# Up projections of a two-layer diffusion backbone in groups of four output tiles, half of the row blocks by seven products of quarters

## The chip, the cores and the metric

One core of one Trainium2 chip runs the whole program. The metric is the device time of one execution in microseconds (us). The kernel before takes 1343.74 us, the median of three runs (1343.1 to 1344.23).

The engines are named as in the profile: PE is TensorE (matmul), PEld its weight loads, DVE VectorE, ACT ScalarE, POOL GpSimd, and SP the queue that issues most transfers.

## The reference

Two trunk layers work on 512 latent tokens of width 1024, the first also on 256 context tokens. Each layer is a mixer and then a gated channel mixer, and the change is in the channel mixer's first product (`w_up`, 1024 x 5632):

```python
def modulate(h, shift, scale):
    return h * (1.0 + scale[:, None, :]) + shift[:, None, :]

def conv_ffn(h, w_up, conv_w, conv_b, w_down):
    a, val = jnp.split(h @ w_up, 2, axis=-1)
    return (jax.nn.gelu(dwconv3(a, conv_w, conv_b), approximate=False) * val) @ w_down

for layer in range(2):
    mod = silu(c) @ ada_w[layer] + ada_b[layer]
    shift_m, scale_m, gate_m, shift_f, scale_f, gate_f = jnp.split(mod, 6, axis=-1)
    ...   # layer 0: neighbourhood attention and a gated recurrence; layer 1: a gated short convolution
    x = x + gate_m[:, None, :] * y
    h = modulate(rms_norm(x, norm_ffn_w[layer]), shift_f, scale_f)
    x = x + gate_f[:, None, :] * conv_ffn(h, ffn_w_up[layer], ...)
return rms_norm(x, final_norm_w)
```

All data is float32. `dwconv3` is a convolution of three taps along the tokens.

## The kernel before, in words

Everything is kept transposed: a tile has 128 features on the partitions and 512 tokens along the free axis, so that h is 8 tiles (`src[k]`, k = 0 to 7), each as a high part and a low part in fp32r. A product of float32 is made of three fp32r matmuls (`mm3`: high by high, weight high by low, weight low by high), and w_up is 22 output tiles for a and 22 for val.

`Weights` streams the weights. `_load` brings a chunk of 1 MB into one of two `wraw` buffers through the SP queue; `conv` makes from half a chunk (128x1024, one output tile) the high part by a cast on ACT (L84, `whi`, three buffers) and the low part by a subtraction on DVE (L85, `wlo`, three buffers). The plan fixes the order of the chunks, `ahead` how far the casts run in front of the matmuls.

`ffn_up` goes over j = 0 to 10, each time two tiles of a and two of val. For j = 0 `quad` does the four tiles in halves of 256 tokens, while the norm ahead still writes h. For the other ten, `pair` does two tiles of a (48 matmuls of 512 columns), then, after the convolution and gelu of a have been issued, `pair` does two of val. The convolution `conv3` is one activation on ACT (L1079, Identity with scale and bias) and two scalar_tensor_tensor on DVE (L1080, L1081), gelu is on ACT (L1108), the product with val on DVE (L1116), and `split` makes the high part (ACT, L242) and the low part (DVE, L243) that the down projection reads. All of these read PSUM directly. The accumulators are four PSUM banks that `acc_t` hands out in turn.

`units(n)` issues n small steps of the modulation vectors between the products: each `ada.unit` loads 256 KB of `ada_w` (`ar`, tag `araw`) and does one DVE instruction of 512 columns with it (L460, L462); every eighth is followed by a reduction (L466), a small matmul (L472) and four small additions (L478). There are 160 such steps in all. They are issued in `project_back`, in the up projections and in the odd mixer.

The Tile framework schedules the instructions of each engine within the order in which they are written and inserts the semaphores; each engine executes its own queue in order.

Of the kernel before, what the change touches and what calls it, by code (L numbers as in the profile page):

```python
# [9 lines left out]
F32 = mybir.dt.float32  # L10
# [8 lines left out]
P = 128  # L19
# [19 lines left out]
class Weights:  # L39


    def __init__(self, nc, pool, plan):
        self.nc, self.pool, self.plan = nc, pool, plan
        self.subs = [(c, s) for c, (_, subs) in enumerate(plan) for s in range(len(subs))]
        self.raw = {}
# [19 lines left out]
    def conv(self):  # L65

        if self.nsub >= len(self.subs):
            return
        c, s = self.subs[self.nsub]
        while self.nload <= min(c + 1, len(self.plan) - 1):  # L70
# [12 lines left out]
        rv = self.raw[c][i][:, k0:k1, c0:c1]  # L83
        self.nc.scalar.copy(hv, rv)  # L84
        self.pin(self.nc.vector.tensor_tensor(lv, rv, hv.bitcast(F32), ALU.subtract))  # L85
        self.ready.append((hv, lv))
        self.nsub += 1

    def ahead(self, n):
# [44 lines left out]
def backbone(ctx: ExitStack, tc: tile.TileContext, a, out, dump=None):  # L134
# [23 lines left out]
    def cols(w, c0):  # L158
        return [([ktiled(w)[:, :, c0 : c0 + 256]], [(0, 0, w.shape[0] // P, j, j + P) for j in (0, P)])]
# [21 lines left out]
        plan += cols(w_out, 256 * j)  # L181

    def ffn_up_plan(l):
        r = []
        for j in range(FT // 2):
            r += cols(up[l], 256 * j) + cols(up[l], FF + 256 * j)
        return r

    plan += ffn_up_plan(0)
# [51 lines left out]
    def split(hi, lo, src):  # L241
        S.copy(hi, src)  # L242
        V.tensor_tensor(lo, src, hi.bitcast(F32), ALU.subtract)  # L243
# [188 lines left out]
    class Ada:  # L432
# [560 lines left out]
    def project_back(nm, src, groups, gate, norm, start=0):  # L993
# [67 lines left out]
    def quad(nm, src, rest):  # L1061
# [13 lines left out]
        ws.pin = lambda i: i  # L1075
        return o[:2], o[2:]

    def conv3(t, src, w0, w1, w2, b):
        S.activation(t[:], src, AF.Identity, scale=w1, bias=b)  # L1079
        V.scalar_tensor_tensor(t[:, 1:], src[:, : T - 1], w0, t[:, 1:], ALU.mult, ALU.add)  # L1080
        V.scalar_tensor_tensor(t[:, : T - 1], src[:, 1:], w2, t[:, : T - 1], ALU.mult, ALU.add)  # L1081
# [8 lines left out]
    def units(n):  # L1090
        for _ in range(n):
            ada.unit(aux_t)

    def ffn_up(l, src, rest):
        g = []
        for j in range(FT // 2):
            if j == 0:
                oa, ov = quad(f"a{l}", src, rest)
            else:
                oa = pair(f"a{l}{j}", src)  # L1100
                units(1 + l)
            t = []
            for i in range(2):
                f = 2 * j + i
                col = lambda n: fcv[l][:, n : n + 1]
                tt = fp.tile([P, T], F32, tag="t", name=f"cv{l}{f}", bufs=5)
                conv3(tt, oa[i], col(f), col(22 + f), col(44 + f), col(66 + f))
                S.activation(tt[:], tt[:], AF.Gelu)  # L1108
                t.append(tt)
            if j:  # L1110
                ov = pair(f"v{l}{j}", src)
                units(1 + l)
            for i in range(2):
                f = 2 * j + i
                gh, gl = gtiles(l, f)
                V.tensor_tensor(ov[i][:], ov[i][:], t[i][:], ALU.mult)  # L1116
                split(gh, gl, ov[i][:])
                g.append((gh, gl))
        return g

    mix = [mixn[p_] for p_ in range(4)] + [mixg[h] for h in range(4)]
# [22 lines left out]
    for j in range(4):  # L1144
        if j == 0:
            oc, ou = quad("c", nrm.h, rest)
        else:
            oc = pair(f"c{j}", nrm.h)
            units(2)
        cs = []  # L1150
        for i in range(2):
            t = gp.tile([P, T], F32, tag=f"g{16 + i}", name=f"cs{j}{i}")
# [1 line left out]
            cs.append(t)  # L1154
        if j:
            ou = pair(f"u{j}", nrm.h)
            units(2)
        ts_ = []
        for i in range(2):
            m = 2 * j + i  # L1160
# [5 lines left out]
        units(2)  # L1166
# [18 lines left out]
    for k2 in range(2):  # L1185
        pt = aux_t(f"pgb{k2}")
        for k in range(4):
            dg = fp.tile([P, P], F32, tag="dg", name=f"dgb{k2}{k}", bufs=2)
# [60 lines left out]
def layout(inputs):  # L1249
# [4 lines left out]
                                "od_conv_w", "ada_b")]  # L1254
    for l in range(2):
        vecs += [inputs["ffn_conv_w"][l], inputs["ffn_conv_b"][l]]
    arrays["vec"] = np.ascontiguousarray(np.concatenate([np.asarray(v).reshape(-1, P) for v in vecs], 0).T)
    rpb = np.asarray(inputs["na_rpb"])[0].reshape(4, 2, 15, 31)
    rp = np.zeros((4, 15, 2, WPAD), rpb.dtype)
# [29 lines left out]
```

## Time and profile before

| what | value |
|---|---|
| median of three runs | 1343.74 us |
| the profiled execution's own time | 1343.25 us |
| its span, first to last instruction | 1341.5 us |
| busy share PE / PEld / DVE / ACT / POOL | 98 / 84 / 61 / 39 / 6 % |
| granted TensorE clock | 0.999 |
| up projections j = 1 to 10, layer 0 | 441.14 to 661.40 us of the span |
| the down projection of layer 0 behind them | 661.4 to 784.9 us |
| the odd mixer | 784.9 to 918.1 us |
| up projections j = 1 to 10, layer 1 | 985.90 to 1206.50 us |
| the down projection of layer 1 | 1206.5 to 1336 us |

The span is the execution as the profiler sees it; 1.75 us of the execution's time lie outside it. A row of a timeline has the start, the duration, the engine, the source line, what is written and read, and in brackets how long the engine was idle before and what released it. A row of the grouped views has busy time in all, the mean of one in ns, and the idle time before.

### The profile page before, as it was taken

Reading aid. Unit: us, or ns where it says so; the run is one execution under the profiler, and the core shown is the slowest. Engines: PE = TensorE matmul, PEld = TensorE weight load, DVE = VectorE, ACT = ScalarE, POOL = GpSimd, SP = SyncE. Lnnn points to the kernel's source line nnn. Section 1 sums busy time; section 2 is a strip of 40 time slices with the busy share of each in tenths; the row PEclk is TensorE's granted clock in tenths of the full one; section 3 lists DMA queues with packets and bytes.
Section 4 is the critical chain, followed back from the end, with each engine's and each line's share of the span. In section 5 each row is a group of like instructions: output and inputs, shape, how many; then the busy total and the mean of one; then the engine's idle time right before and its main releaser. Section 6 shows DMA issues by size and latency. Waiting matters only on the chain. (4 is left out here: it accounts for less than half of the span.)

```text
span 1341.5 us, 19127 instructions
## 1 busy us (share of the span) xinstructions
PE 1318.2 (98%) x7736; PEld 1126.1 (84%) x7736; DVE 821.3 (61%) x1354; ACT 527.9 (39%) x815; POOL 84.4 (6%) x87
## 2 busy tenths in 40 slices
PE   7999999999999999999999999999999999999997
PEld 4798888888779888888888898888988888889997
DVE  4668897887777655555566666557676444442333
ACT  4443445555544433333322243223543333333223
POOL 2204332311000000000000000000000000000000
PEclk9999999999999999999999999999999999999999
DMA  9842113674562333334366624445333233332231
GB/s 290 266 125 80 32 32 85 149 188 132 151 196 95 118 118 118 118 118 126 123 205 196 206 95 141 141 144 168 128 95 120 97 100 103 101 99 73 88 110 63
DMA packets 170825, 172.21 MB, mean 128 GB/s; under 512 B 14321, under 2 KB 144753, under 8 KB 170737
## 3 DMA queue, kind: packets, MB, share of 16 engines
q1 hardware_dynamic: 168736, 166.15, 40.1%
q10 hardware_dynamic: 2000, 4.85, 1.4%
q8 instruction: 60, 0.98, 0.3%
q14 instruction: 29, 0.23, 0.1%
HBM read 165.21 MB, written 2.10 MB: 125 GB/s over the span
## 5 line engine op out<-in xcount | busy, mean ns | idle before, releaser
L84 ACT CAST whi<-wraw 128x1024 fp32r<-128x1024 f32 (+1 forms) x202 | 207.7, 1031 | 469.2 <-PE ppv L247 93.4
L85 DVE TENSOR_TENSOR wlo<-wraw,whi 128x1024 fp32r<-128x1024 f32 (+1 forms) x202 | 243.5, 1207 | 217.8 <-ACT whi L84 216.5
L247 PE MATMUL ppa<-hf,whi 128*128 128x512 f32 (+1 forms) x448 | 161.6, 361 | 0.0
L246 PE MATMUL ppa<-hf,whi 128*128 128x512 f32 (+1 forms) x448 | 161.2, 360 | 0.0
L248 PE MATMUL ppa<-hf,wlo 128*128 128x512 f32 (+1 forms) x448 | 160.2, 358 | 0.0
L247 PE MATMUL ppv<-hf,whi 128*128 128x512 f32 x320 | 126.1, 394 | 0.0
L246 PE MATMUL ppv<-hf,whi 128*128 128x512 f32 x320 | 125.8, 393 | 0.0
L248 PE MATMUL ppv<-hf,wlo 128*128 128x512 f32 x320 | 124.3, 388 | 0.0
L462 DVE SCALAR_TENSOR_TENSOR aa<-ar,sil,aa 128x512 f32<-128x512 f32 x140 | 105.4, 753 | 17.4 <-DMA ar<-in_ada_w_dram 15.9
L1205 PE MATMUL pd<-whi,g 128*128 128x256 f32 x352 | 98.1, 279 | 0.0
L1207 PE MATMUL pd<-wlo,g 128*128 128x256 f32 x352 | 98.0, 278 | 0.0
L1206 PE MATMUL pd<-whi,g 128*128 128x256 f32 x352 | 97.7, 278 | 0.0
L246 PEld LDWEIGHTS ppa<-hf,whi 128*128 128x128 f32 x448 | 84.1, 188 | 13.9
L248 PEld LDWEIGHTS ppa<-hf,wlo 128*128 128x128 f32 x448 | 84.1, 188 | 13.2
L247 PEld LDWEIGHTS ppa<-hf,whi 128*128 128x128 f32 x448 | 84.2, 188 | 12.2
L1116 DVE TENSOR_TENSOR ppv<-ppv,cv 128x512 f32<-128x512 f32 x40 | 28.0, 700 | 86.0 <-PE ppv L248 86.0
L246 PE MATMUL pbd<-g,whi 128*128 128x512 f32 (+1 forms) x192 | 72.3, 377 | 0.0
L247 PE MATMUL pbd<-g,whi 128*128 128x512 f32 (+1 forms) x192 | 72.0, 375 | 0.0
L248 PE MATMUL pbd<-g,wlo 128*128 128x512 f32 (+1 forms) x192 | 71.7, 373 | 0.0
L246 PEld LDWEIGHTS ppv<-hf,whi 128*128 128x128 f32 x320 | 60.1, 188 | 13.8
L248 PEld LDWEIGHTS ppv<-hf,wlo 128*128 128x128 f32 x320 | 60.1, 188 | 13.4
L247 PEld LDWEIGHTS ppv<-hf,whi 128*128 128x128 f32 x320 | 60.2, 188 | 11.9
(340 smaller groups left out, 2862.3 us busy)
## 6 DMA issues: line engine op xcount, KB each, us to landing
wraw<-in_ffn_w_up_dram SPq DMA_DIRECT2D x44, 1024.0 KB, 5.1
ar<-in_ada_w_dram SPq DMA_DIRECT2D x160, 256.0 KB, 2.9
wraw<-in_ffn_w_down_dram SPq DMA_DIRECT2D x16, 1024.0 KB, 5.1
wraw<-in_od_w_in_dram SPq DMA_DIRECT2D x12, 1024.0 KB, 5.3
wraw<-in_ev_w_in_dram SPq DMA_DIRECT2D x20, 512.0 KB, 5.3
araw<-in_ada_w_dram SPq DMA_DIRECT2D x16, 512.0 KB, 6.5
wraw<-in_ffn_w_down_dram SPq DMA_DIRECT2D x8, 768.0 KB, 5.2
wraw<-in_ev_w_out_dram SPq DMA_DIRECT2D x4, 1024.0 KB, 7.3
```

Of the source, the lines that this page charges most:

```text
L84: self.nc.scalar.copy(hv, rv)
L85: self.pin(self.nc.vector.tensor_tensor(lv, rv, hv.bitcast(F32), ALU.subtract))
L246: TE.matmul(o, wh, mh, start=start, stop=False, skip_group_check=True)
L247: TE.matmul(o, wh, ml, start=False, stop=False, skip_group_check=True)
L248: TE.matmul(o, wl, mh, start=False, stop=stop, skip_group_check=True)
L462: pin(V.scalar_tensor_tensor(self.acc[:], raw[:], sil[:, r, 0:1], self.acc[:], ALU.mult, ALU.add))
L1116: V.tensor_tensor(ov[i][:], ov[i][:], t[i][:], ALU.mult)
L1205: TE.matmul(o[i][:, 0:256], gh[:, ts], w[0][:, k - k0], start=k == 0, stop=False)
L1206: TE.matmul(o[i][:, 0:256], gl[:, ts], w[0][:, k - k0], start=False, stop=False)
L1207: TE.matmul(o[i][:, 0:256], gh[:, ts], w[1][:, k - k0], start=False, stop=k == FT - 1)
```

## The change

For j = 1 to 10 `group` replaces the two `pair` calls. The four output tiles of one j are taken as two columns of a 2x2 block scheme: m = 0 and m = 1 are the two tiles of a and of val, the tokens are two halves (A: 0 to 255, B: 256 to 511), and the row blocks k = 0 to 3 are two pairs. The product of these quarters is done by seven products instead of eight, in Winograd's form, with sums of weights (S1 to S4) and sums of activations (T1 to T4). The row blocks k = 4 to 7 are done plainly, as W1 and W2 (the weights of m = 0 and m = 1) by XA and XB (the two halves of the activations). Each of the seven products is 12 matmuls of 256 columns, each of the four plain ones 24: 180 matmuls of 256 columns, where `pair` twice had 96 of 512.

The partial results share the banks a, b, c and d, and have to be combined: ACT copies bank contents to SBUF tiles `R` (L1180, eight copies of 128x256 for one j), and DVE adds other banks to them (L1176, eight of 128x256). Bank b is copied after S2·T2 while S3·T3 has still to be added to it. The convolution, gelu, product and split (now L1212, L1213, L1214, L1235, L1237, L281, L282) read and write R in SBUF.

The weights come from a new array `upq` that the host lays out: a chunk of quarters (A21, A22, A11, A12) and a chunk of W1 and W2. `_block` makes S3, S1, S2 and S4 on DVE (L105, L107, L109, L111; the last three in place in the raw tile), and casts and subtracts each (L122 on ACT, L123 on DVE). `differences` makes T2 to T4 once a layer, `first` T1. `units` moves: none in the up projections of layer 0, two after each of the groups j = 1 to 8 in layer 1, five instead of four in `project_back` where the rows come in several groups, and three instead of two in the odd mixer; `araw` has two buffers instead of three.

```diff
@@ Weights.conv, and the new _block
+        nm = self.plan[c][1][s]
+        while self.nload <= min(c + 1 + (nm == "W2"), len(self.plan) - 1):
             self._load()
+        if isinstance(nm, str):
+            self._block(c, nm)
+            return
...
+    HOME = {"A11": ("a", 0), "S1": ("a", 1), "A12": ("b", 0), "W1": ("c", None), "S2": ("d", 0), "S4": ("d", 1),
+            "S3": ("e", 0), "A22": ("e", 1), "W2": ("f", None)}
+    def _block(self, c, nm):
+        quarters = self.raw[c][0]
+        A21, A22, A11, A12 = (quarters[:, 0, 512 * i : 512 * i + 512] for i in range(4))
+        if nm == "S1":
+            s3 = self.pool.tile([P, 512], F32, tag="ws3", name=f"ws3{self.nsub}", bufs=1)
+            V.tensor_tensor(s3[:], A11, A21, ALU.subtract)
+            self.half["S3"] = s3[:]
+            V.tensor_tensor(A21, A21, A22, ALU.add)
+        elif nm == "S2":
+            V.tensor_tensor(A21, A21, A11, ALU.subtract)
+        elif nm == "S4":
+            V.tensor_tensor(A21, A12, A21, ALU.subtract)
...
+        if z in (None, 0):
+            self.half[key] = [self.pool.tile([P, 1024], F32R, tag=t, name=f"{t}{self.nsub}", bufs=3) for t in ("whi", "wlo")]
+        at = 512 * (z or 0)
+        hi, lo = (t[:, at : at + src.shape[-1]] for t in self.half[key])
+        self.nc.scalar.copy(hi, src)
+        V.tensor_tensor(lo, src, hi.bitcast(F32), ALU.subtract)
...
@@ ffn_up_plan
+        r = cols(up[l], 0) + cols(up[l], FF)
+        for j in range(FT // 2 - 1):
+            q = [a["upq"][l, j, i][:, None, :] for i in range(2)]
+            r += [([q[0]], ["A11", "S1", "A12", "W1", "S2", "S4", "S3", "A22", "W2"]), ([q[1]], [])]
@@ ada
-            raw = ap_.tile([P, T], F32, tag="araw", name=f"ar{n}", bufs=3)
+            raw = ap_.tile([P, T], F32, tag="araw", name=f"ar{n}", bufs=2)
-            while len(self.raw) < min(self.n + 3, 8 * len(self.jobs)):
+            while len(self.raw) < min(self.n + 2, 8 * len(self.jobs)):
@@ project_back
-                units(4)
+                units(4 if len(groups) == 1 else 5)
@@ the new group
+    def group(nm, mv):
+        bank = {n: acc_t(f"p{n}{nm}") for n in "bcad"}
+        R = [[fp.tile([P, T], F32, tag=t, name=f"R{nm}{t}", bufs=1) for t in ("sqa", "Rv")],
+             [fp.tile([P, T], F32, tag=t, name=f"R{nm}{t}", bufs=1) for t in ("r", "Rw")]]
...
+        upto(4)
+        product("b", "A11", "B11", True)
+        product("c", "S1", "T1", True)
+        copy("b", 0, A)
+        upto(5)
+        product("a", "A12", "B21", True)
+        copy("c", 1, B)
+        upto(7)
+        product("a", "W1", "XA", False, True)
+        upto(8)
+        product("c", "W1", "XB")
+        add("a", 0, A)
+        product("b", "S2", "T2")
+        upto(9)
+        product("c", "S4", "B22", False, True)
+        copy("b", 0, B)
+        product("b", "S3", "T3")
+        add("c", 0, B)
+        yield R[0]
+        upto(11)
+        add("b", 1, B)
+        product("b", "A22", "T4")
+        upto(12)
+        product("b", "W2", "XA", False, True)
+        product("d", "W2", "XB", True, True)
+        copy("b", 1, A)
+        add("d", 1, B)
+        yield R[1]
@@ ffn_up
-                oa = pair(f"a{l}{j}", src)
-                units(1 + l)
-                ov = pair(f"v{l}{j}", src)
-                units(1 + l)
+        for j in range(1, FT // 2):
+            for i, (ra, rv) in enumerate(group(f"{l}{j}", mv[0])):
+                gated_tile(2 * j + i, ra, rv)
+            if l and j < 9:
+                units(2)
```

`gated_tile` holds the convolution, gelu, product and split of one pair of tiles, as before. The other edits are the odd mixer's `units(3)`, one buffer instead of two for a tile `dg` of the last norm, the host's layout of `upq`, and a smaller scratch area for GpSimd's transfers.

In the order of PE, the place where bank b is copied and added to again reads as follows in the third group of layer 0 (T_4582 and T_4583 are T2 and T3, whi_5341/wlo_5342 hold S2 and then S4, whi_5362/wlo_5363 S3 and then A22, and whi_5310/wlo_5311 W1).

```order
L285 MATMUL pb_5302<-T_4582,whi_5341 128x256
L286 MATMUL pb_5302<-T_4582,whi_5341 128x256
L287 MATMUL pb_5302<-T_4582,wlo_5342 128x256
L285 MATMUL pb_5302<-T_4583,whi_5362 128x256
L286 MATMUL pb_5302<-T_4583,whi_5362 128x256
L287 MATMUL pb_5302<-T_4583,wlo_5363 128x256
...
L285 MATMUL pb_5302<-T_4583,whi_5362 128x256
L285 MATMUL pc_5303<-hf_4136,whi_5310 128x256
```

S3·T3 stands right behind S2·T2 in the same bank, seven of its twelve matmuls ahead of the 24 of W1·XB in bank c. In the kernel before, PE went from one bank to another at this place:

```order
L246 MATMUL ppv_5266<-hf_4141,whi_5188 128x512
L247 MATMUL ppv_5266<-hf_4141,whi_5188 128x512
L248 MATMUL ppv_5266<-hf_4141,wlo_5189 128x512
L246 MATMUL ppv_5267<-hf_4134,whi_5256 128x512
L247 MATMUL ppv_5267<-hf_4134,whi_5256 128x512
```

Nothing between these rows had to be copied first. On ACT, the rows around the same place of the changed kernel follow; R02 belongs to the group before, R03 to this one, and cv_5293 and g_5298 are the gated tile of the group before.

```order
L1180 COPY R02r<-pb_5041 128x256
L1180 COPY R02Rw<-pb_5041 128x256
L1212 ACTIVATE cv_5293<-R02r,vec 128x512
L122 CAST whi_5362<-ws_5218 128x512
L122 CAST whi_5362<-wraw_5169 128x512
L122 CAST whi_5341<-wraw_5169 128x512
L1235 ACTIVATE cv_5293<-cv_5293 128x512
L1180 COPY R03r<-pc_5303 128x256
L281 CAST g_5298<-R02Rw 128x512
L1180 COPY R03sqa<-pb_5302 128x256
L1180 COPY R03Rv<-pb_5302 128x256
```

The two copies of bank b in the last rows stand behind the whole gated tile of the group before and the cast L281 of its product. On ACT before, a cast of weights and a step of the gated tile took turns:

```order
L84 CAST whi_5329<-wraw_5186 128x1024
L242 CAST g_5319<-ppv_5266 128x512
L84 CAST whi_5335<-wraw_5260 128x1024
L242 CAST g_5324<-ppv_5267 128x512
L84 CAST whi_5404<-wraw_5260 128x1024
L1079 ACTIVATE cv_5394<-ppa_5339,vec 128x512
```

On DVE, this is what stands ahead of the product R02Rw that the cast L281 reads, and what follows it:

```order
L111 TENSOR_TENSOR wraw_5169<-wraw_5169 128x512
L1214 SCALAR_TENSOR_TENSOR cv_5293<-R02r,vec,cv_5293 128x511
L123 TENSOR_TENSOR wlo_5363<-ws_5218,whi_5362 128x512
L123 TENSOR_TENSOR wlo_5342<-wraw_5169,whi_5341 128x512
L1237 TENSOR_TENSOR R02Rw<-R02Rw,cv_5293 128x512
L123 TENSOR_TENSOR wlo_5363<-wraw_5169,whi_5362 128x512
L1176 TENSOR_TENSOR R03sqa<-pa_5304,R03sqa 128x256
L282 TENSOR_TENSOR g_5298<-R02Rw,g_5298 128x512
L1176 TENSOR_TENSOR R03Rv<-pa_5304,R03Rv 128x256
L105 TENSOR_TENSOR ws_5480<-wraw_5430 128x512
L123 TENSOR_TENSOR wlo_5433<-wraw_5212,whi_5432 128x1024
```

The product L1237 comes behind the difference S4 and two low parts, and the next chunk's quarters (wraw_5430) stand ahead of W2's low part. Before, DVE had one low part of 128x1024 for each product:

```order
L1116 TENSOR_TENSOR ppv_5266<-ppv_5266,cv_5246 128x512
L85 TENSOR_TENSOR wlo_5330<-wraw_5186,whi_5329 128x1024
L243 TENSOR_TENSOR g_5320<-ppv_5266,g_5319 128x512
L1116 TENSOR_TENSOR ppv_5267<-ppv_5267,cv_5251 128x512
L85 TENSOR_TENSOR wlo_5336<-wraw_5260,whi_5335 128x1024
L243 TENSOR_TENSOR g_5325<-ppv_5267,g_5324 128x512
```

There, one low part of the weights stands between two steps of the gated tiles.

More of the change, by code (lines that the diff above doesn't have):

```diff
@@ L44, in __init__ @@
         self.subs = [(c, s) for c, (_, subs) in enumerate(plan) for s in range(len(subs))]
+        self.half = {}
         self.raw = {}
@@ L86, in conv @@
         self.ready.append((hv, lv))
+        self.nsub += 1
+    HOME = {"A11": ("a", 0), "S1": ("a", 1), "A12": ("b", 0), "W1": ("c", None), "S2": ("d", 0), "S4": ("d", 1),
+            "S3": ("e", 0), "A22": ("e", 1), "W2": ("f", None)}
+    def _block(self, c, nm):
+        V = self.nc.vector
+        quarters = self.raw[c][0]
[9 more added lines that the diff above has]
+            V.tensor_tensor(A21, A12, A21, ALU.subtract)
+        if nm in ("W1", "W2"):
+            at = 1024 * (nm == "W2")
+            src = self.raw[c + 1][0][:, 0, at : at + 1024]
+        else:
+            src = {"A11": A11, "A12": A12, "A22": A22, "S3": self.half.get("S3")}.get(nm, A21)
+        key, z = self.HOME[nm]
+        if z in (None, 0):
[4 more added lines that the diff above has]
+        V.tensor_tensor(lo, src, hi.bitcast(F32), ALU.subtract)
+        self.ready.append(tuple(t.rearrange("p (g k c) -> p g k c", g=2, c=P) for t in (hi, lo)))
         self.nsub += 1
@@ new lines, in group, with product, upto, add @@
+    def group(nm, mv):
+        bank = {n: acc_t(f"p{n}{nm}") for n in "bcad"}
+        v = {n: t[:].rearrange("p (g t) -> p g t", g=2) for n, t in bank.items()}
+        R = [[fp.tile([P, T], F32, tag=t, name=f"R{nm}{t}", bufs=1) for t in ("sqa", "Rv")],
+             [fp.tile([P, T], F32, tag=t, name=f"R{nm}{t}", bufs=1) for t in ("r", "Rw")]]
+        base = ws.ncall
+        order = ["A11", "S1", "A12", "W1", "S2", "S4", "S3", "A22", "W2"]
+        w = {}
+        A, B = HALF
+        def product(n, wn, xn, first=False, last=False):
+            while wn not in w:
+                w[order[len(w)]] = ws.get(0)
+            wh, wl = w[wn]
+            nk = wh.shape[2]
+            for g_ in range(2):
+                for k in range(nk):
+                    mh, ml = mv[xn](k)
+                    mm3(v[n][:, g_], wh[:, g_, k], wl[:, g_, k], mh, ml, first and g_ == 0 and k == 0,
+                        last and k == nk - 1)
+        def upto(n):
+            ws.ahead(base + n - ws.ncall)
+        def add(n, m, c):
+            for g_ in range(2):
+                r = R[m][g_][:, c]
+                V.tensor_tensor(r, v[n][:, g_], r, ALU.add)
+        def copy(n, m, c):
+            for g_ in range(2):
+                S.copy(R[m][g_][:, c], v[n][:, g_])
+        upto(4)
[26 more added lines that the diff above has]
+        yield R[1]
@@ L1095, in ffn_up, with gated_tile, before @@
         g = []
[L1096 to L1099, printed above, removed]
-                oa = pair(f"a{l}{j}", src)
-                units(1 + l)
[L1102 to L1110, printed above, removed]
-                ov = pair(f"v{l}{j}", src)
-                units(1 + l)
[L1113 to L1118, printed above, removed]
+        mv = []
+        def gated_tile(f, oa, ov):
+            col = lambda n: fcv[l][:, n : n + 1]
+            tt = fp.tile([P, T], F32, tag="t", name=f"cv{l}{f}", bufs=5)
+            conv3(tt, oa, col(f), col(22 + f), col(44 + f), col(66 + f))
+            S.activation(tt[:], tt[:], AF.Gelu)
+            gh, gl = gtiles(l, f)
+            V.tensor_tensor(ov[:], ov[:], tt[:], ALU.mult)
+            split(gh, gl, ov[:])
+            g.append((gh, gl))
+        def before():
+            rest()
+            mv.extend(differences(l, src))
+        oa, ov = quad(f"a{l}", src, before)
+        mv[1]()
+        for i in range(2):
+            gated_tile(i, oa[i], ov[i])
+        for j in range(1, FT // 2):
[3 more added lines that the diff above has]
+                units(2)
         return g
```

44 lines of the change are left out of this document (35 added, 9 removed).

## The prediction, made before the changed kernel was run

> **What bounds the kernel now.** I read the page's first section, then the busy time of each engine by stretches, then the timelines of PE, DVE and ACT in the third group of layer 0 (times in us).
>
> ```profile
> span 1341.5 us, 19127 instructions
> PE 1318.2 (98%) x7736; PEld 1126.1 (84%) x7736; DVE 821.3 (61%) x1354; ACT 527.9 (39%) x815; POOL 84.4 (6%) x87
> ```
>
> The second row gives busy time, share and instructions: PE is nearly always busy. By stretches (length; then busy time and instructions of PE, PEld, DVE, ACT and POOL, granted clock, DMA share, GB/s):
>
> ```profile
> 441.14:661.40 220.26, 220.26 (x968) 180.83 (x967) 122.80 (x161) 82.25 (x107) 0.00 (x0) 1.00 0.39 122
> 985.90:1206.50 220.60, 220.60 (x970) 181.13 (x969) 117.76 (x150) 82.85 (x108) 0.00 (x0) 1.00 0.33 107
> 661.40:784.90 123.50, 123.50 (x590) 102.96 (x589) 79.48 (x121) 35.22 (x43) 0.00 (x0) 1.00 0.63 201
> ```
>
> In the two stretches that the change rewrites PE has no gap at all, and DVE works 122.80 of 220.26 us. So one j costs 22.04 us (the mean of 22.03 and 22.06), and whatever takes matmuls away gains, if the rest keeps up. The durations of PE follow, first of 512 columns, then of 256 (the quad):
>
> ```profile
> 463.35 0.39 PE L246 MATMUL ppa<-hf,whi 128*128 128x512 f32 x1
> 474.34 0.39 PE L246 MATMUL ppv<-hf,whi 128*128 128x512 f32 x1
> ...
> 428.54 0.28 PE L248 MATMUL ppa<-hf,wlo 128*128 128x256 f32 x1
> 439.99 0.28 PE L248 MATMUL ppa<-hf,wlo 128*128 128x256 f32 x1
> L246 PEld LDWEIGHTS ppa<-hf,whi 128*128 128x128 f32 x448 | 84.1, 188 | 13.9
> ```
>
> Between the first two lie 48 matmuls: 10.99/48 = 0.229 each. Between the next two lie 99: 11.45/99 = 0.1157, a little over half. A matmul of 256 columns is recorded for 0.28, so its result is there 0.16 after the next could start.
>
> **The change, PE first.** Out go 96 matmuls of 512 columns for each j, in come 180 of 256: 180 x 0.1157 = 20.83, 1.21 less than 22.04. Over 20 groups that is 24 us, if PE never waits. Whether it waits is decided by ACT and DVE, which have one queue each. Their prices, from the timelines (idle time and releaser in brackets) and from the groups (busy, mean ns | idle):
>
> ```profile
> 475.39 1.22 DVE L85 TENSOR_TENSOR wlo<-wraw,whi 128x1024 fp32r<-128x1024 f32 x1 [2.82 <-ACT whi L84]
> 476.53 0.74 DVE L1080 SCALAR_TENSOR_TENSOR cv<-ppa,vec,cv 128x511 f32<-128x511 f32 x1
> 477.19 0.74 DVE L462 SCALAR_TENSOR_TENSOR aa<-ar,sil,aa 128x512 f32<-128x512 f32 x1
> 477.85 0.74 DVE L1081 SCALAR_TENSOR_TENSOR cv<-ppa,vec,cv 128x511 f32<-128x511 f32 x1
> 480.03 0.70 DVE L1116 TENSOR_TENSOR ppv<-ppv,cv 128x512 f32<-128x512 f32 x1 [1.44 <-PE ppv L248]
> 487.52 0.69 DVE L243 TENSOR_TENSOR g<-ppv,g 128x512 fp32r<-128x512 f32 x1
> 488.12 0.74 DVE L462 SCALAR_TENSOR_TENSOR aa<-ar,sil,aa 128x512 f32<-128x512 f32 x1
> ...
> 474.31 1.05 ACT L84 CAST whi<-wraw 128x1024 fp32r<-128x1024 f32 x1 [1.01 <-PE ppa L247]
> 478.69 0.63 ACT L1108 ACTIVATE cv<-cv 128x512 f32<-128x512 f32 x1 [2.65 <-DVE cv L1081]
> ...
> 479.60 0.39 PE L248 MATMUL ppv<-hf,wlo 128*128 128x512 f32 x1
> L1212 DVE TENSOR_TENSOR yt<-pd,gb 128x256 f32<-128x256 f32 x16 | 6.5, 421 | 18.5 <-PE pd L1207 18.5
> L1079 ACT ACTIVATE cv<-ppa,vec 128x512 f32<-128x512 f32 x44 | 34.1, 775 | 18.0 <-PE ppa L248 18.0
> L586 ACT COPY ckt<-pkc 128x256 f32<-128x256 f32 x8 | 3.0, 371 | 28.2 <-PE pkc L584 28.2
> L242 ACT CAST QS<-qn 64x512 fp32r<-64x512 f32 x8 | 4.9, 617 | 0.2
> ```
>
> On DVE the next instruction starts about 0.08 before the record of the last ends: 1.14 for 1024 columns, 0.66 for a scalar_tensor_tensor of 511, 0.60 for a tensor_tensor of 512 (487.52 to 488.12), and by the same cut 0.34 for 256 (421 ns recorded). On ACT, by the same cut of about 0.09, it is 0.28 for a copy of 256 columns (371) and 0.53 for a cast of 512 (617). Handing over: ACT to DVE 0.03 (475.36 to 475.39), DVE to ACT 0.10 (478.59 to 478.69), PE to DVE 0.04 (479.99 to 480.03).
>
> Per group DVE has two low parts of 1024, fifteen tensor_tensors of 512 (seven lows, four differences, two products, two splits), four scalar_tensor_tensors and eight adds of 256: 2.28 + 9.00 + 2.64 + 2.72 = 16.6, against 12.28 a j before (122.80/10), which included the steps of the modulation vectors. It fits into 20.8 as a sum. ACT likewise stays under two thirds. So no engine is the bound; the order within the queues is.
>
> **Where PE waits.** S3·T3 adds to bank b, so its first matmul must wait for the two ACT copies R03sqa and R03Rv of that bank. They stand behind cast L281 of the last group's product, which waits for DVE's L1237. I put zero at the start of the last matmul of the previous group's W2·XA and follow the queues as they are ordered:
>
> - DVE: W1's low part waits for that matmul to free its buffer, 0.28 + 0.04 = 0.32, next at 1.46. S2's low part to 2.06.
> - ACT: a cast of 512 from 0.20 to 0.73 (its buffer is freed by W2's last high part), the two copies of bank b to 1.29, identity L1212 to 2.07.
> - DVE: first scalar_tensor_tensor from 2.10, S4 from 2.76, second from 3.36, low part of S3 from 4.02, of S4 from 4.62, L1237 from 5.22, recorded to 5.92. (Gelu, from 4.11 + 0.10 to 4.84 on ACT, is in time.)
> - ACT: cast L281 at 6.01, the copies at 6.51 and 6.79, ended at 7.16. PE may start S3·T3 at 7.20.
> - PE: one matmul of S1·T1, 12 of A12, 24 of W1·XA, 12 of S2·T2 lie between, so it is free at 50 x 0.1157 = 5.79.
>
> PE waits 1.41. Had ACT been free, the copies would still cost 0.16 + 0.04 + 0.28 + 0.37 + 0.04 = 0.9 here: that is the floor of this term, 1.41 the value I take, since every step of it has its row.
>
> The Trainium skill speaks to this, in "Perfetto Trace Analysis", section Optimizing Tensor Performance: independent groups of matmuls should rotate through PSUM banks, so that emptying one overlaps the next, and larger matmuls are better than smaller ones. The trace before agrees (banks alternate and PE has no gap), and no run here yet shows the other case. By that rule the change goes wrong exactly at S3·T3; with a bank of its own the sum would be 1.41 a group less.
>
> Two smaller waits follow. DVE's first difference L105 of the next group waits for the quarters, and W2's low part stands behind it. The raw tile is free when A22's low part is done, 5.82 + 0.69 = 6.51; the transfer then takes as long as this one of the same size:
>
> ```profile
> wraw<-in_ffn_w_up_dram SPq DMA_DIRECT2D x44, 1024.0 KB, 5.1
> ```
>
> So it lands at 6.53 + 5.1 = 11.63; L105 to 12.25, W2's low part ends 13.48. PE wants it 52 matmuls after 7.20, at 13.22: it waits 0.3. The second half of the low part for S1 stands behind two adds, one low part, two scalar_tensor_tensors, L107 and an add: DVE reaches it at about 16.93 and ends it at 17.62; PE wants it at 17.43: 0.2. All the rest of what is added (differences, other copies and adds, split) ends ahead of its reader by 0.1 or more, or is read a group later. The bounds of these two: nothing if the quarters, now in rows of 8 KB where they were of 1 KB, land 0.9 sooner; later than 5.1 is the second rival below.
>
> One group: 20.83 + 1.41 + 0.3 + 0.2 = 22.75, against 22.04. Twenty groups: +14.2. With 0.1135 to 0.118 for a matmul and 0.9 to 2.2 of waits it is 21.3 to 23.4, -14 to +28.
>
> **The other parts.** The first group behind each quad inherits its tiles:
>
> ```profile
> 441.18 0.75 DVE L1080 SCALAR_TENSOR_TENSOR cv<-ppa,vec,cv 128x511 f32<-128x511 f32 x1 [8.01 <-ACT cv L1079]
> 443.73 1.28 ACT L1108 ACT_TABLE_LOAD   x1
> ```
>
> DVE idles 8 us inside the quad, which covers `differences` (on DVE four sums, three low parts of 512 and eight differences of 256: 7 x 0.60 + 8 x 0.34 = 6.9). Behind the quad two identities, four scalar_tensor_tensors, the table load of 1.28 and two products now stand ahead of the first group's low parts: I reckon 2 us a layer, +4, between 0 and +8. In the down projection of layer 0 five steps of the modulation vectors for four, on two buffers instead of three:
>
> ```profile
> DMA to landing us min/median/max: 2.6/3.0/6.4
> DVE aa L462 <- DMA ar<-in_ada_w_dram: 15.9, 17, 2.4
> ```
>
> The first row is that stage's; with three buffers DVE already waited 17 times for a step's data over the span, 2.4 at most. DVE has 44 of 123.5 us to spare there, and PE waits only where it uses this up: 0 to +5, I take +1. The steps removed from layer 0's up projections free DVE for nothing that PE wanted, and those moved into layer 1's fall where DVE waits for quarters. In the odd mixer DVE keeps its spare time, and `dg` is a moment: both nothing.
>
> Sum: 14.2 + 4 + 1 = +19.2 on the profiled execution's own 1343.25 (span 1341.5 and 1.75 around it; the median of the runs is 0.5 higher): 1362.5, about 1.4% slower.
>
> **Rivals.**
>
> - *The count of matmuls decides* (faster). PE sees fewer of these waits than I reckoned: if the waits of a group stay under 22.04 - 20.83 = 1.21, it gains. With only the floor of 0.9 it is 21.73, -6; with the scheduler's overlap perfect, -24; with 2 to 4 us of the quads, 1321 to 1341, most likely 1335. For it: my chain of nine steps need only be 0.3 shorter than I think, and the two small waits vanish with a faster transfer. Against it: each step has its row, and the queues run in order.
> - *The quarters come late* (slower still). Their raw tile is freed only after S4 and A22 have been used, so the transfer can't run ahead. If it takes 6.4 (the slowest landing of a step's 256 KB, above) instead of 5.1, DVE passes 1.3 on to W2's low part in every group: 20 x 1.3 = 26 more, 1388. For it: DVE reads the tile first in its queue. Against it: 5.1 is the median of 44.
> - *Weight loads bound the smaller matmuls.* 180 loads of 0.188 (the row of PEld) would make 33.8 a group, (33.8 - 22.04) x 20 = +235, 1579. Against it: in the quad each matmul of 256 columns has its load, and they are 0.1157 apart. The Trainium skill, "TensorE: Matmul & The Clock Gate", section Back-to-back issue gap, says that the spacing is set by load and matmul together, pipelined; the quad shows that here they overlap.
>
> **How the numbers follow.** The forecast, 1347 to 1382, has 0.58; the gain 0.26; late quarters 0.09; bound by loads 0.01; and 0.06 is left for no change. The measurement can tell about 0.2% from nothing, 2.7 us. So faster 0.26, same 0.06, slower 0.68. For the range I leave out what lies above 1384 (late quarters, loads) and the best part of the gain, below 1328.
>
> **What would show it.** In the profile after: 180 matmuls a group at 0.115 to 0.116; a gap of PE at the first matmul of S3·T3, released by ACT's copy R..Rv, of 0.9 to 1.5, twenty times; smaller gaps at W2 into bank d, released by DVE's low part, whose own wait is for L105's transfer; a group of 22.3 to 23.2. I am wrong if the gap at S3·T3 is under 0.9 or lies elsewhere, if the quarters land well under 5 us, or if the first groups and the down projection take more than 8 us together.

## The result and the profile after

The changed kernel takes 1374.82 us (median of four runs, 1372.33 to 1376.03), the kernel before 1343.42 (four runs): a ratio of 1.0231, interval 1.0214 to 1.0249. It is slower by 31.4 us; 19.2 were forecast, and the forecast's range, 1347 to 1382, holds the time. One of the twelve executions of the last kernel in the experiments below took 1596.78 us at a granted clock of 0.752, and the time given there leaves it out. The first lines of the page after:

```profile
span 1372.8 us, 23237 instructions
PE 1320.2 (96%) x9416; PEld 1196.2 (87%) x9416; DVE 969.7 (71%) x1728; ACT 629.7 (46%) x1085; POOL 83.6 (6%) x87
```

PE's busy time hardly changed although matmul columns were saved (a record of 256 columns is 0.28 long where the next starts after 0.12, so that a wait of less than 0.16 shows as no gap), and PE's share fell from 98 to 96%. The stretches that answer to those before (columns as there): the groups of layer 0, its down projection, the odd mixer, and the groups of layer 1.

```profile
445.28:674.27 228.99, 218.10 (x1810) 214.65 (x1809) 172.60 (x295) 128.32 (x232) 0.00 (x0) 1.00 0.26 92
674.27:806.44 132.17, 125.86 (x588) 103.60 (x586) 84.53 (x130) 36.64 (x46) 0.00 (x0) 0.99 0.63 203
806.44:941.80 135.36, 134.28 (x684) 114.06 (x683) 93.00 (x150) 43.91 (x62) 0.00 (x0) 1.00 0.49 151
1009.76:1240.00 230.24, 219.89 (x1824) 216.05 (x1823) 181.69 (x318) 128.40 (x232) 0.00 (x0) 1.00 0.28 100
```

PE now has gaps in all four. The start of the quad of layer 0 tells that something was lost even ahead of the groups; the first row is of the kernel before, the second of after:

```profile
418.43 0.28 PE L246 MATMUL ppa<-hf,whi 128*128 128x256 f32 x1
422.50 0.28 PE L285 MATMUL ppa<-hf,whi 128*128 128x256 f32 x1
```

By stages, each from its first matmul, as in such rows (before, the down projection goes from 661.58 to 785.01 and the odd mixer to 918.29; after, 1.18 us of the down projection stand inside the groups of layer 0 and are counted with it):

| stage | forecast | measured |
|---|---|---|
| up to the quad of layer 0 | 0 | +4.1 |
| groups of layer 0, with the first | +9.1 | +7.4 |
| down projection of layer 0 | +1 | +9.9 |
| odd mixer | 0 | +2.1 |
| its output projection and the quads | 0 | +0.4 |
| layer 1 from the groups to the end | +9.1 | +7.4 |
| span | +19.2 | +31.3 |

The last row but one is known to about 3 us only: the last down projection takes 127.6 us in the kernel before and 131.0 and 128.3 in the first two of the experiments, which change nothing in its products. The groups came out near what was worked out, and half of the loss, 16.5 of 31.3 us, lies elsewhere. The third group of layer 0, in the timelines of DVE, ACT and PE:

```profile
498.20 0.69 DVE L1237 TENSOR_TENSOR R02Rw<-R02Rw,cv 128x512 f32<-128x512 f32 x1
504.35 0.69 DVE L105 TENSOR_TENSOR ws<-wraw 128x512 f32<-128x512 f32 x1 [3.59 <-DMA wraw<-in_upq_dram]
...
498.92 0.62 ACT L281 CAST g<-R02Rw 128x512 fp32r<-128x512 f32 x1 [0.85 <-DVE R02Rw L1237]
499.45 0.37 ACT L1180 COPY R03sqa<-pb 128x256 f32<-128x256 f32 x1
499.71 0.38 ACT L1180 COPY R03Rv<-pb 128x256 f32<-128x256 f32 x1
...
498.72 0.28 PE L287 MATMUL pb<-T,wlo 128*128 128x256 f32 x1
500.14 0.39 PE L285 MATMUL pb<-T,whi 128*128 128x256 f32 x1 [1.14 <-ACT R03Rv L1180]
```

With the prediction's zero at 492.95, L1237 starts at 5.25 (5.22 forecast) and S3·T3 at 7.19 (7.20). PE starts nothing for 1.42 us, 1.30 more than a matmul takes. This stands in nine groups of layer 0 and in six of layer 1; three more of layer 1 have a gap of 0.6 to 0.9 us there, and the first group of each layer has none. The copies that end one group and start the next give the period; the first and the last of eight:

```profile
493.68 0.36 ACT L1180 COPY R02r<-pb 128x256 f32<-128x256 f32 x1
653.59 0.36 ACT L1180 COPY R09r<-pb 128x256 f32<-128x256 f32 x1
```

159.91/7 = 22.84 a group, 22.75 forecast. In layer 1 the same copies are 22.80 to 22.89 us apart four times and then 23.20 to 23.61 four times; what adds the half microsecond there stays open.

### The profile page after: what moved, and what is told of

Read it like the earlier page. It is cut to its first block, busy times and chain, and to the rows that moved or that the text cites. A ratio compares the mean times of both kernels' runs of the same rounds, so it can differ in the third digit from the quotient of the medians.

```text
span 1372.8 us, 23237 instructions
## 1 busy us (share of the span) xinstructions
PE 1320.2 (96%) x9416; PEld 1196.2 (87%) x9416; DVE 969.7 (71%) x1728; ACT 629.7 (46%) x1085; POOL 83.6 (6%) x87
## 5 line engine op out<-in xcount | busy, mean ns | idle before, releaser
L89 ACT CAST whi<-wraw 128x1024 fp32r<-128x1024 f32 (+1 forms) x122 | 124.1, 1021 | 279.0 <-PE pbd L286 70.2
L90 DVE TENSOR_TENSOR wlo<-wraw,whi 128x1024 fp32r<-128x1024 f32 (+1 forms) x122 | 144.9, 1190 | 106.0 <-ACT whi L89 102.0
L122 ACT CAST whi<-wraw 128x512 fp32r<-128x512 f32 (+1 forms) x160 | 116.5, 729 | 139.2 <-PE pc L286 69.3
L123 DVE TENSOR_TENSOR wlo<-wraw,whi 128x512 fp32r<-128x512 f32 (+1 forms) x160 | 129.5, 821 | 49.7 <-PE pb L287 32.3
L287 PE MATMUL pc<-hf,wlo 128*128 128x256 f32 x320 | 91.1, 285 | 0.7 <-DVE wlo L123 0.7
L285 PE MATMUL pc<-hf,whi 128*128 128x256 f32 x320 | 89.3, 279 | 0.0
L286 PE MATMUL pc<-hf,whi 128*128 128x256 f32 x320 | 89.3, 279 | 0.0
L285 PE MATMUL pb<-T,whi 128*128 128x256 f32 x240 | 69.2, 288 | 19.3 <-ACT R05Rv L1180 1.1
L287 PE MATMUL pa<-hf,wlo 128*128 128x256 f32 x240 | 67.4, 281 | 0.9 <-DVE wlo L123 0.9
L285 PE MATMUL pb<-hf,whi 128*128 128x256 f32 x240 | 67.8, 283 | 0.0
L286 PE MATMUL pb<-T,whi 128*128 128x256 f32 x240 | 67.2, 280 | 0.0
L286 PE MATMUL pb<-hf,whi 128*128 128x256 f32 x240 | 67.1, 280 | 0.0
L285 PE MATMUL pa<-hf,whi 128*128 128x256 f32 x240 | 67.1, 280 | 0.0
L286 PE MATMUL pa<-hf,whi 128*128 128x256 f32 x240 | 67.0, 279 | 0.0
```

Of the source, the lines that this page charges most:

```text
L122: self.nc.scalar.copy(hi, src)
L285: TE.matmul(o, wh, mh, start=start, stop=False, skip_group_check=True)
L286: TE.matmul(o, wh, ml, start=False, stop=False, skip_group_check=True)
L287: TE.matmul(o, wl, mh, start=False, stop=stop, skip_group_check=True)
```

## The experiments

All are timed against the kernel before on the same chip; ratios with their 95% interval. Beside the changed kernel the kernel before took 1343.42 us, beside the runs below 1343.88 to 1346.15, so a difference of 1 or 2 us from the changed kernel is better read from the ratios. The runs ask two things: where the loss outside the groups comes from, and what sets the period inside.

**Two buffers alone.** The kernel before, with

```diff
-            raw = ap_.tile([P, T], F32, tag="araw", name=f"ar{n}", bufs=3)
+            raw = ap_.tile([P, T], F32, tag="araw", name=f"ar{n}", bufs=2)
-            while len(self.raw) < min(self.n + 3, 8 * len(self.jobs)):
+            while len(self.raw) < min(self.n + 2, 8 * len(self.jobs)):
```

> The kernel before with only the buffers of the modulation steps (araw) cut from three to two. Mine: what the change lost outside its groups comes with the buffers and the moved steps. The transfers of the position bias stand behind the steps' loads in SP's queue, so the mixer of layer 0 ends about 4 us later; in the down projection of layer 0, with four steps a weight pair still, DVE's waits for step data go from 7.8 to about 15 us, and PE loses 0 to 4. Sum +4 to +9: 1347 to 1352 us. Rival: the loss outside belongs to the groups (their late results, the other transfers); then nothing moves, 1342 to 1346.

Measured 1349.36 against 1343.88 us, ratio 1.0042 (1.0027 to 1.0057). The quad starts late by 4.4 us, about as much as in the changed kernel, and the down projection of layer 0 is untouched:

```profile
422.80 0.28 PE L246 MATMUL ppa<-hf,whi 128*128 128x256 f32 x1
...
665.94:789.46 123.52, 123.52 (x590) 103.00 (x589) 80.06 (x121) 35.28 (x43) 0.00 (x0) 1.00 0.63 200
```

So the buffer costs what the mixer of layer 0 lost, and four steps on two buffers cost the down projection nothing (123.43 before). DVE's waits for the steps' data rose there from 7.9 to 23.9 us, more than expected, and PE waited for none of it.

**The moved steps too.** The same, with the change's other places:

```diff
-                units(4)
+                units(4 if len(groups) == 1 else 5)
-                units(1 + l)          # twice in ffn_up
+                if l and j < 9:       # once, behind val
+                    units(2)
-            units(2)                  # three times in the odd mixer
+            units(3)
```

> The kernel before with two buffers and also the moved steps of the change (none in layer 0's up projections, two per j in layer 1's, five instead of four in the down projection of layer 0, three instead of two in the odd mixer), without the groups. Mine: all that the change lost outside the groups, +4 in the mixer of layer 0, +9 in the down projection of layer 0, +2 in the odd mixer: 1356 to 1361 us. Rival (the groups are the cause): less than +3, under 1347.

Measured 1357.32 us, ratio 1.0102 (1.0082 to 1.0121): 13.4 us are lost without a single group. Down projection and odd mixer:

```profile
664.89:797.40 132.51, 127.03 (x593) 104.09 (x592) 85.81 (x135) 34.53 (x42) 0.00 (x0) 0.99 0.62 199
797.40:932.96 135.56, 134.11 (x684) 113.91 (x683) 91.81 (x147) 43.83 (x62) 0.00 (x0) 1.00 0.48 148
```

+9.1 and +2.3, near the +9.9 and +2.1 of the changed kernel. The rival, that the groups cause it, is out.

What PE waits for in the down projection of the changed kernel stands in these rows (time in all, times, longest), and behind them two stretches near its end:

```profile
PE pad L511 <- DVE ad L505: 5.2, 5, 2.4
PE pbd L285 <- DVE xT L999: 1.1, 1, 1.1
...
798.70:800.70 2.00, 2.00 (x14) 2.00 (x15) 1.50 (x7) 0.72 (x2) 0.00 (x0) 0.77 0.90 273
800.70:803.00 2.30, 2.30 (x13) 2.30 (x12) 1.09 (x2) 0.01 (x1) 0.00 (x0) 0.50 0.35 105
```

L511 is the small matmul behind eight steps; it needs the reduction L505 on DVE and stands in PE's queue, so all of the down projection waits with it. These 6.3 us of gaps, and about 1.6 us by a granted clock of 0.77 and 0.50 behind the last two of them, make most of the 9.9. PE waits behind no low part there.

**Three buffers in the changed kernel**, paid for by one buffer of the tag `t`.

> The changed kernel with three buffers for the steps' data again, paid for by one buffer of the tag t (four instead of five). Mine: the mixer of layer 0 loses its 4 us again, and of the 9 us in the down projection 4 to 8 go, since DVE waits less for the data of five steps: 1362 to 1367 us. Rival (not the buffers): 1373 to 1377.

Measured 1367.6 us, ratio 1.0177 (1.0162 to 1.0192), 7.2 less than after and 0.6 above what I expected. The quad starts at 419.13, so the mixer has its time back, and the odd mixer too, though it still has three steps a product:

```profile
801.38:934.77 133.39, 133.39 (x684) 113.62 (x683) 89.18 (x141) 42.89 (x61) 0.00 (x0) 1.00 0.45 141
```

The down projection has not. There DVE still waited 14 times, 19.5 us, for five steps' data, and one wait cost more than its length. PE's timeline and its stretches (granted clock is the third number from the right):

```profile
719.47 0.58 PE L511 MATMUL pad<-ad,cst 128*128 128x16 f32 x2 [4.92 <-DVE ad L505]
720.46 0.63 PE L285 MATMUL pbd<-g,whi 128*128 128x512 f32 x1
723.02 0.63 PE L285 MATMUL pbd<-g,whi 128*128 128x512 f32 x1
723.99 0.39 PE L285 MATMUL pbd<-g,whi 128*128 128x512 f32 x1
...
719.40:723.40 4.00, 3.93 (x10) 3.24 (x11) 3.34 (x8) 1.05 (x1) 0.00 (x0) 0.50 0.65 180
```

L511 waited 4.92 us, and the matmuls behind it ran at half the clock for 3.5 us: six matmuls from 720.46 to 723.02 are 0.427 apart, not 0.23.

**The steps put back** in the changed kernel, on two buffers:

```diff
-            if l and j < 9:
+            if j < 9 or not l:
                 units(2)
-                units(4 if len(groups) == 1 else 5)
+                units(4)
-            units(3)                  # three times in the odd mixer
+            units(2)
```

> The changed kernel with the modulation steps nearly where they were before: two per group in layer 0's up projections (j below 10 too), four instead of five in the down projection, two instead of three in the odd mixer; still two buffers. Mine: the fifth step is what the down projection pays for (its transfers share a queue and 16 engines with the weights), so 7 to 9 us go there and 2 in the odd mixer, and the groups of layer 0 keep their 22.85, since DVE does the steps while it waits for quarters, as in the groups j = 1 to 4 of layer 1: 1364 to 1367 us. Rival: the two buffers alone slow any four steps, or the steps lengthen the groups as much: 1371 to 1377.

Measured 1364.01 us, ratio 1.0134 (1.0114 to 1.0154). The down projection (1.86 us of which now stand in the last group):

```profile
675.98:798.55 122.57, 122.22 (x584) 101.70 (x582) 80.41 (x122) 37.19 (x47) 0.00 (x0) 1.00 0.65 208
```

It has lost its gaps, and the groups of layer 0 kept their 22.8 to 23.0 with two steps each. So the place of the steps is the cause there, not the buffers: four fit between two pairs of weights, five don't. Why five don't stays open. DVE waits for the steps' data about as long with four steps on two buffers (first row) as with five (second row):

```profile
DVE aa L462 <- DMA ar<-in_ada_w_dram: 21.7, 18, 3.1
DVE aa L501 <- DMA ar<-in_ada_w_dram: 25.3, 18, 3.4
```

What differs is how near the reduction comes to the small matmul that reads it. Before, PE reaches that matmul 3.3 us or more after the reduction has ended; in the changed kernel PE is there first, and it starts within 0.15 us of the end. The source issues it three steps behind the reduction, which is less time when a pair of weights has five steps. Late data and this short distance may both count; no run separates them.

**The position bias from ACT's queue.** One word, `nc.sync` to `nc.scalar` for its transfers.

> The changed kernel with the transfers of the position bias issued from ACT's queue instead of SP's. If the 4 us in the mixer of layer 0 come from these transfers standing behind the steps' loads in SP's queue, they go: 1370 to 1372 us. If they come from the steps' data themselves, nothing: 1373 to 1377.

Measured 1379.12 us, ratio 1.0246 (1.0223 to 1.0269): no gain, and the quad starts at 427.95, 5.4 us later still. So this doesn't decide how the missing buffer delays the mixer. That it does is shown by taking the buffer away and by giving it back; by which wait stays open. Its size varies: in all other profiles the quad starts at 420.5 to 423.3 with two buffers (seven kernels) and at 418.4 to 420.3 with three (five), so that 4 us is a high value.

**S3·T3 held back.** The matmuls of S4·B22 and S3·T3 kept in the order of the source:

```diff
-                    mm3(..., last and k == nk - 1)
+                    mm3(..., last and k == nk - 1, pin if wn in ("S4", "S3") else (lambda i: i))
```

> The changed kernel with S3·T3 held behind S4·B22 in PE's queue, as the source has it, so that 36 matmuls stand between S2·T2 and it. If the wait at S3·T3 is lost time by itself, it goes and nothing takes its place: 20 x 1.3 = 26 us less, 1347 to 1350 us. If, as I hold, the same chain (DVE's queue, then the transfer of the next quarters, which starts when A22's low part is done) is what sets the period, PE waits next at S1·T1 for its low part, by 0.7 to 1.3 us in a group: 8 to 16 us less, 1358 to 1367 us.

Measured 1394.46 us, ratio 1.0379 (1.036 to 1.0398): 20 us *slower* than after, and both expectations missed. Its timelines of PE, ACT and DVE in the fourth group:

```profile
523.59 0.39 PE L285 MATMUL pc<-hf,whi 128*128 128x256 f32 x1 [1.80 <-ACT R04Rw L1180]
...
521.36 0.62 ACT L281 CAST g<-R03Rw 128x512 fp32r<-128x512 f32 x1 [0.33 <-DVE R03Rw L1237]
522.14 0.38 ACT L1180 COPY R04Rv<-pb 128x256 f32<-128x256 f32 x1
523.16 0.37 ACT L1180 COPY R04Rw<-pc 128x256 f32<-128x256 f32 x1 [0.64 <-DVE g L282]
...
522.45 0.68 DVE L282 TENSOR_TENSOR g<-R03Rw,g 128x512 fp32r<-128x512 f32 x1
```

S3·T3 no longer waits, but what stands in its place does: W1·XB needs bank c copied, that copy goes into tile Rw, and Rw has one buffer, which is free only when the split L282 of the last group has read it. In the changed kernel the wait at S3·T3 had covered this one, since W1·XB stands behind it there.

**A second buffer for Rw**, paid for by one of the tag `t`; first with S3·T3 held back, then without:

```diff
-             [fp.tile([P, T], F32, tag=t, name=f"R{nm}{t}", bufs=1) for t in ("r", "Rw")]]
+             [fp.tile([P, T], F32, tag=t, name=f"R{nm}{t}", bufs=1 + (t == "Rw")) for t in ("r", "Rw")]]
```

> S3·T3 behind S4·B22 as in the run before, and a second buffer for the result tile Rw (paid for by one buffer of the tag t), so that the copy of bank c need not wait for the split L282 of the last group. If the one buffer of Rw made W1·XB wait (1.8 us a group), that wait goes; by the queues PE then waits about 0.5 at S3·T3 (its copies stand behind the cast of W2 on ACT) and 0.8 at S1·T1 (the quarters' transfer still starts only after A22's low part): a group of 22.0 to 22.4, 1358 to 1367 us. If that buffer isn't the cause, W1·XB waits on and the time stays at 1390 to 1396.

> The changed kernel with the second buffer for Rw and one less of the tag t, and the order of PE as in the changed kernel. Control for the run above: the copies of bank b wait for L281, not for a buffer, so the wait at S3·T3 stays at 1.3 and the group at 22.85: 1373 to 1377 us. If instead the buffer of Rw is what holds the period, it falls by 5 us or more.

Measured 1357.53 us, ratio 1.0078 (1.0052 to 1.0104), and 1360.75, ratio 1.0114 (1.0097 to 1.0132). The first time is 0.5 below what I expected, with groups of 22.03, but not for the reason given: PE does not wait at S3·T3; it waits up to 0.3 at W1·XB for the copy of bank c and up to 0.6 at S1·T1. The second was meant as a control and fell too, by 14 us, since its order of PE is not that of the changed kernel: with Rw free, the scheduler itself puts W1·XB between the first matmuls of S2·T2 and the rest, and S3·T3 behind S4·B22. Its period and its wait for the quarters:

```profile
491.50 0.37 ACT L1180 COPY R02r<-pb 128x256 f32<-128x256 f32 x1
645.94 0.36 ACT L1180 COPY R09r<-pb 128x256 f32<-128x256 f32 x1
...
DVE ws L105 <- DMA wraw<-in_upq_dram: 6.8, 15, 1.4
```

154.44/7 = 22.06 a group, 0.78 less. In the changed kernel that wait for the quarters was this:

```profile
DVE ws L105 <- DMA wraw<-in_upq_dram: 51.5, 18, 3.8
```

So S3·T3 stood where PE had to wait for it because W1·XB, which could have filled the time, had no tile to copy its bank to. The four combinations of order and buffer bear it out: with one buffer 1374.82 and 1394.46 us, with two 1360.75 and 1357.53. The one buffer of Rw is behind both waits.

**All three mended, and two steps more.** `Rw` from the five buffers of the tag `t`, which leaves room for the third `araw` buffer, and the steps put back:

> The changed kernel with all three losses mended: the result tile Rw taken from the five buffers of tag t (so that it has more than one), which frees the room for the third buffer of the steps' data, and the steps' places as in a_steps_back. If the three causes are separate and add up (two buffers 4 us, fifth step and odd mixer 11, Rw's one buffer 14), this gives 1374.8 - 4 - 10.8 - 14 = 1346: 1343 to 1349 us, with groups of 22.0 to 22.1. If they overlap or another cause is behind them, 1351 us or more.

Measured 1346.19 us, ratio 1.0009 (0.9998 to 1.0020), where the sum gave 1346, with groups of 22.14: the three causes nearly add up. By the ratios, the third buffer, the steps and Rw alone gained 0.54, 0.97 and 1.17% on the changed kernel, 2.68 together, and all three gained 2.22. The odd mixer's 2 us (0.15%) is in the first two; what is left is about what the intervals allow. Then the tile `r` from tag `t` as well:

> As g_all_mended, and the result tile r from tag t as well, so that both copies of bank c come ahead of gelu on ACT and W1·XB right behind W1·XA. If the copies of bank c are what PE waits for at W1·XB (0.3 to 0.5 a group), 4 to 9 us less than g_all_mended: 1336 to 1342 us. If the quarters' transfer sets the period, no change.

Measured 1342.59 us, ratio 0.9985 (0.9974 to 0.9995): 3.6 less, 0.6 above what I expected. Then `upto(11)` ahead of `yield R[0]`:

> As g_two_result_tiles, and the weights A11 and S1 of the next group are asked for ahead of the first gated tile in the source, which puts the sum for S1 and its low part earlier in DVE's queue by a scalar_tensor_tensor and a product (1.2 us). If PE waits at S1·T1 for that low part (0.5 to 0.9 a group), 6 to 14 us less than g_two_result_tiles: 1325 to 1336 us, faster than the kernel before. If something else holds the period, no change.

Measured 1342.89 us, ratio 0.9979 (0.9966 to 0.9991), no change from the one before it and far from the gain I expected. Its period, first and last of eight:

```profile
490.03 0.37 ACT L1180 COPY R02tu<-pb 128x256 f32<-128x256 f32 x1
643.44 0.37 ACT L1180 COPY R09tu<-pb 128x256 f32<-128x256 f32 x1
```

153.41/7 = 21.92, against 20.83 by the count of matmuls, or 21.06 at the 0.117 us apart that they are in the groups. PE's waits there are small and in changing places (up to 0.4 us behind low parts, adds of R and the steps' additions); I have not taken them apart further. By their ratios these two are faster than the kernel before by 0.15 and 0.21%, about what can be told from nothing.

## Why the prediction was right, and where it was off

The direction and the wait that was to decide the groups came out as forecast. That the time lies in the range is in part luck. The range is 35 us wide; 16.5 us were lost in stages that had been put at +1 together, and the groups with the first ones came out 3.4 below their forecast. The last of the prediction's own signs of being wrong, more than 8 us in the first groups and the down projection together, came true by the down projection alone.

- *PE's count, and that the order of the queues decides.* Right. No engine is full, and waits and a slower pace took more than the 24 us that the count saves. The matmuls of 256 columns in the groups are 0.117 apart (the twelve of S2·T2 that end with the row at 498.72 began at 497.43) where I put 0.1157: 0.3 a group.
- *The wait at S3·T3.* Right in place and size: 1.41 forecast, 1.30 measured, eighteen times instead of twenty. The chain's points lie within 0.04 us of the rows (with a slip of 0.03 in them, since 6.01 and 0.53 make 6.54 and not 6.51); PE came 0.1 later than forecast, at 5.89, which is the difference.
- *The two small waits*, 0.5 together. 22.84 less 180 x 0.117 less 1.30 leaves 0.5, but not where I put it. W2's low part was in time within 0.1 (L105 at 11.40 instead of 11.65, since the quarters land in 4.8 instead of 5.1), that of S1 within 0.2, and 0.1 comes from the first matmul behind the long wait, which the next follows after 0.23 (500.14 to 500.37 us).
- *What the wait was worth.* Here my reading of cause was short. I said that ACT's place of the copies makes PE wait; holding S3·T3 back showed a second reader of the same chain behind it, and a buffer as the reason for both. That a wait is the one that ends last doesn't say that removing it gains.
- *The first groups*, +4. Too high: with them the groups of each layer lost 7.4, where ten full groups at 0.80 make 8.0 without any extra. So the first groups cost nothing that shows.
- *The down projection of layer 0*, +1, bounds 0 to +5. This is the step that failed: +9.9. I said that PE waits only where DVE's spare time (44 us) is used up. It is not: DVE is busy 84.53 of 132.17 us after, and PE waits all the same, 5.2 us for the reduction that L511 reads and 1.1 for an addition of the last result, with a slower clock behind. I took the price from the total of idle time, not from the interval of 11 us in which one pair's weights and five steps, their reduction and its reader have to follow each other. That the steps' new places are the cause is shown; whether the fifth step's data come too late or the reduction stands too near L511 is open.
- *The mixer of layer 0*, no term: +4.1. I looked for the cost of the missing buffer only where steps were added. The kernel has 58 steps ahead of the quad, and they lost the buffer too.
- *The odd mixer*, nothing: +2.1. PE waits 1.1 us at its start for low parts of its input, which stand in DVE's queue. With the third buffer back, or with the steps put back, the loss is gone (133.4 and 133.1 us against 133.3), so it takes both.
- *The rival of late quarters*: not so; they land sooner than before. *Bound by weight loads*: PEld is busy 214.65 of 228.99 us in the groups and yet matmuls are 0.117 apart where nothing waits, so the loads were no bound. *The gain by count* is not reached even in the last run: 21.92 a group, 0.12 less than before.
- The Trainium skill's rule ("Perfetto Trace Analysis", section Optimizing Tensor Performance), that groups of matmuls should rotate through PSUM banks, named the right place. The runs add that the target of the copy must rotate as well: with the same four banks and one more result tile no wait at S3·T3 is left, one of up to 0.3 us stands at W1·XB, and a group takes 22.06 us instead of 22.84.

## What to carry to other kernels

Before a change that adds results to be kept, write down for each buffer who frees it and when, and look for the next reader behind the wait you found: mend one and the other takes its place. A buffer or a step taken away to make room is paid for everywhere it is used, so cost it in each stage, over the interval of one iteration, not in a stage's total of spare time. And run the change without its main part: here that alone told half of the loss from the other half.

## What the runs showed of the hardware

A wait of PE can cost twice. After 4.92 us of waiting the granted clock was 0.50 for about 3.5 us (above); after 2.40 us, in the run with the moved steps, it was 0.60 over the next 4.2 us (matmuls of 512 columns about 0.43 apart for 3.4 us of them):

```profile
698.78 0.37 PE L472 MATMUL pad<-ad,cst 128*128 128x16 f32 x2 [2.40 <-DVE ad L466]
698.80:703.00 4.20, 4.20 (x13) 3.34 (x14) 2.60 (x7) 0.00 (x0) 0.00 (x0) 0.60 0.62 219
```

In the changed kernel a wait of 2.37 us was followed by no slower clock:

```profile
753.29 0.37 PE L511 MATMUL pad<-ad,cst 128*128 128x16 f32 x2 [2.37 <-DVE ad L505]
753.30:757.00 3.70, 3.70 (x17) 3.11 (x18) 3.61 (x10) 0.63 (x1) 0.00 (x0) 1.00 0.52 166
```

The Trainium skill ("TensorE: Matmul & The Clock Gate", section What's actually happening) says that the clock halves after at least one idle window of about 3.4 us, is whole again after one busy window of that length, and that the windows run freely. The length of the slow stretches, 3.5 and 3.4 us, agrees. That 2.4 us of waiting can suffice, and can also not, is what these rows add; and near the end of the changed kernel's down projection two waits of 1.06 and 0.93 us within 2.7 us were followed by 0.50 (the rows at 798.70 and 800.70).
